# Splitting once and keeping the halves: latents and output weights of a two-layer attention encoder

## The chip, the cores and the metric

One core of a Trainium2 chip runs the whole program. The metric is device time in microseconds of one execution of the program. The median of three runs of the kernel before is 2840.68 us (2839.82 to 2844.84).

## The reference

Two layers run over 1024 prompt frames and 64 later frames with 256 frames of history, 1088 token rows in all, of width 1024. Everything is float32.

- Layer 0 projects the tokens once into a query latent (768 columns), a key-value latent (256), a rotary key (32) and band queries, keys and values. Both latents are RMS-normed. Eight heads attend over the latents (keys and values are projections of the key-value latent, with a chunk mask), eight heads attend over a band of nine chunks with a relative bias. The two outputs go through one output projection.
- Layer 1 is stick-breaking attention with 16 heads: each weight is a product of sigmoids over the later keys, with no softmax. Its output projection is w_out1.
- After each mixer: add and layer norm, a squared-ReLU feed-forward part of width 4096, add and layer norm.

```
h = x @ w_in
q_a = (rms_norm(h[:, :768], g_q) @ w_uq)       # query latent, then rotary on its last 32 per head
ckv = rms_norm(h[:, 768:1024], g_kv)           # key-value latent
k_a, v_a = ckv @ w_ukv                         # per head 64 key and 64 value columns
```

## The kernel before

**Products in three passes.** A float32 operand x is held as two tiles, H and L: H is x rounded to the matmul's format by a ScalarE copy, L is x minus H by VectorE (`split`, line 137). A product is H*H + H*L + L*H, three matmuls (`mm3`, line 141). Whatever enters a matmul has therefore been split once, by one instruction on each of ScalarE and VectorE. `weight` (line 163) loads one weight piece of up to 128 x 1024 into the single tile `wraw`, then splits it into one of two pairs, `wH0`/`wL0` and `wH1`/`wL1`, taken in turn. All transfers are issued by SyncE (SP), on one queue.

**Order of the work.** The program is written in order, and a planner with a model of the engines then places every engine's instructions; on the chip each engine runs its list strictly in that order. `paced` (line 528) adds ordering edges that the planner obeys but that are no semaphores on the chip.

**Stage 1, `latents` (line 294).** The nine token tiles (eight of 128 rows, one of 64), laid out with the features on the partitions, are loaded and split (`x_piece`); the weights of the key-value latent (`ck_piece`, four pieces) and of the query latent (`ql_piece`, eight) likewise. A first loop over the tiles projects the key-value latent, norms it, stores it as an output, turns it (three transposes), copies it out of PSUM into `stg` and stores it unsplit in the DRAM tensors `ck_d` and `krT_d`. A second loop does the same for the query latent in two halves of 384 columns, into `qn_d`. Then the constant rows of the rotary queries (`qconst`) are split and stored into `qr_d`, twelve transfers. The first band weight, w_bk of pair 0, is asked for inside the second loop.

**Stage 2, band attention.** For four pairs of heads, `heads64` (line 459) projects keys, queries and values of the next pair while `attend` works on the present one. During the last pair `load_latents` brings `qn_d` and `ck_d` back into SBUF, splits them, and splits the rotary key rows with their constants; the query projections (`rotate`, `nope`) fill TensorE's time beside the attention. `rotate` takes its cosine tile, and `parts` its split result, from the three buffers `raw`, which the loads of latents use too.

**Stage 3, latent attention.** `weight(io["w_mv"])` and the value projection come first; `proj_mla` (line 867) loads the key weights of one pair (128 x 256) and projects its keys, one pair ahead of the attention. During the last pair `out_early` (line 985) loads the eight blocks of w_out0, splits them and computes part of the output projection for some tiles.

**Stage 4** is the rest of layer 0 (output projection, feed-forward part). **Stage 5** is layer 1's attention: eight pairs by `heads64` and `row_stick` (line 590), whose chain goes from TensorE (scores) to ScalarE (two sigmoids), VectorE (a scan), GpSimd (a product), TensorE (a transpose), ScalarE and VectorE (split) and TensorE again. During the last pair, once x is released, `out_early` loads and splits w_out1. **Stage 6** is the rest of layer 1.

## Time and profile before

| | |
|---|---|
| median of three runs | 2840.68 us (2839.82 to 2844.84) |
| the profiled execution | 2842.44 us |
| its span, first to last instruction | 2840.6 us |
| TensorE busy | 2737.7 us, 96% |
| VectorE, ScalarE, GpSimd busy | 2160.4, 1512.2, 776.0 us |
| moved by DMA | 335.60 MB |

Stage 1 lasts until about 138 us, the band attention until about 430, layer 1's attention from about 1450 to 2050. PE is TensorE, PEld its weight loads, DVE VectorE, ACT ScalarE, POOL GpSimd, SP SyncE; SPq is SP's queue. L139 is line 139 of the kernel; that line is the subtract of `split`, so its tiles tell which split it is. In a row of groups stand the line, engine, operation and tiles (written<-read), shapes and count, then busy us and mean ns of one, then the engine's idle time before them with what ended it. A matmul's end is modelled, so the start-to-start distance is the better measure of its pace.

### The profile page before, as it was taken

Reading aid. Unit: us, or ns where it says so; the run is one execution under the profiler, and the core shown is the slowest. Engines: PE = TensorE matmul, PEld = TensorE weight load, DVE = VectorE, ACT = ScalarE, POOL = GpSimd, SP = SyncE. Lnnn points to the kernel's source line nnn. Section 1 sums busy time; section 2 is a strip of 40 time slices with the busy share of each in tenths; the row PEclk is TensorE's granted clock in tenths of the full one; section 3 lists DMA queues with packets and bytes.
Section 4 is the critical chain, followed back from the end, with each engine's and each line's share of the span. In section 5 each row is a group of like instructions: output and inputs, shape, how many; then the busy total and the mean of one; then the engine's idle time right before and its main releaser. Section 6 shows DMA issues by size and latency. Waiting matters only on the chain.

```text
span 2840.6 us, 46995 instructions
## 1 busy us (share of the span) xinstructions
PE 2737.7 (96%) x16907; PEld 2499.6 (88%) x16907; DVE 2160.4 (76%) x3837; ACT 1512.2 (53%) x3104; POOL 776.0 (27%) x890
## 2 busy tenths in 40 slices
PE   7999989999999999999999999998999999999998
PEld 7999978887899998878789999998879999977776
DVE  4266684885867777999978888888686777689998
ACT  4266664882555556333247777777445555543331
POOL 3123341652200002222533344344230000122235
PEclk9999999999999999999999999998999999999999
DMA  7122155334243447344231111113242444654442
GB/s 225 51 77 76 56 152 151 84 109 147 98 136 129 148 159 267 118 145 143 82 110 57 46 60 51 51 53 103 78 144 86 159 141 136 230 177 133 158 122 77
DMA packets 235752, 335.60 MB, mean 118 GB/s; under 512 B 45472, under 2 KB 168128, under 8 KB 235520
## 3 DMA queue, kind: packets, MB, share of 16 engines
q1 hardware_dynamic: 235520, 332.61, 37.2%
q8 instruction: 134, 2.20, 0.3%
q14 instruction: 98, 0.80, 0.1%
HBM read 217.83 MB, written 113.33 MB: 117 GB/s over the span
## 4 chain that ended last, share of the span: by engine, by line
PE 78%; DVE 9%; ACT 4%; DMA 4%; issue 3%; POOL 1%; SPq 0%; DVEq 0%; ACTq 0%; POOLq 0%
PE d L143 9%; PE d L144 9%; PE d L145 9%; PE s L143 5%; PE s L145 5%; PE s L144 5%; PE t L143 5%; PE t L144 5%; PE t L145 5%; PE t L161 4%; PE s L542 3%; PE pv L676 2%; PE pv L674 2%; PE pv L145 2%; PE pv L143 2%
## 5 line engine op out<-in xcount | busy, mean ns | idle before, releaser
L610 POOL TENSOR_TENSOR G<-G,S 128x384 f32<-128x384 f32 (+4 forms) x200 | 207.4, 1041 | 347.8 <-DVE S L607 128.4
L143 PE MATMUL d<-xH,wH 128*128 128x384 f32 (+1 forms) x792 | 266.4, 336 | 1.7 <-ACT kraw L509 1.6
L145 PE MATMUL d<-xH,wL 128*128 128x384 f32 (+1 forms) x792 | 264.0, 333 | 1.6 <-DVE wL L139 1.6
L144 PE MATMUL d<-xL,wH 128*128 128x384 f32 (+1 forms) x792 | 264.0, 333 | 0.0
L139 DVE TENSOR_TENSOR wtL<-t,wtH 128x512 fp32r<-128x512 f32 (+2 forms) x328 | 196.8, 618 | 54.3 <-ACT wtH L138 47.1
L138 ACT ACTIVATE wtH<-t 128x512 fp32r<-128x512 f32 (+2 forms) x328 | 170.6, 545 | 64.4 <-PE t L161 32.8
L549 POOL TENSOR_TENSOR R<-R,inv 128x640 f32<-128x640 f32 (+6 forms) x100 | 118.7, 1195 | 185.5 <-DVE inv L548 117.6
L674 PE MATMUL pv<-wtH,V 128*128 128x256 f32 (+1 forms) x624 | 159.3, 280 | 8.3 <-ACT o L634 4.0
L676 PE MATMUL pv<-wtL,V 128*128 128x256 f32 (+1 forms) x624 | 155.2, 289 | 7.0 <-DVE wtL L139 7.0
L143 PEld LDWEIGHTS d<-xH,wH 128*128 128x128 f32 x792 | 150.1, 190 | 5.4 <-ACT kraw L509 2.7
L607 DVE TENSOR_TENSOR_SCAN S<-S,own 128x513 f32<-128x513 f32 (+3 forms) x144 | 143.9, 1006 | 13.8 <-ACT S L600 12.2
L145 PEld LDWEIGHTS d<-xH,wL 128*128 128x128 f32 x792 | 149.9, 189 | 3.2 <-DVE wL L139 1.8
L144 PEld LDWEIGHTS d<-xL,wH 128*128 128x128 f32 x792 | 149.9, 189 | 1.0
L138 ACT ACTIVATE wo<-wo 128x1024 fp32r<-128x1024 f32 (+4 forms) x100 | 87.9, 883 | 113.9 <-DMA wo<-a_d 21.4
L674 PEld LDWEIGHTS pv<-wtH,V 128*128 128x128 f32 x624 | 120.1, 192 | 13.7 <-ACT o L634 6.3
L676 PEld LDWEIGHTS pv<-wtL,V 128*128 128x128 f32 x624 | 120.0, 192 | 10.8 <-DVE wtL L139 9.6
L161 PE MATMUL t<-ident,G 128*128 128x128 f32 x600 | 107.4, 282 | 12.6 <-POOL G L610 6.4
L542 PE MATMUL s<-kS,qH 128*128 128x384 f32 (+3 forms) x288 | 106.4, 372 | 4.9 <-ACT G L601 2.7
L600 ACT ACTIVATE S<-s 128x384 f32<-128x384 f32 (+4 forms) x200 | 99.1, 495 | 12.3 <-PE s L542 8.7
L601 ACT ACTIVATE G<-s 128x384 f32<-128x384 f32 (+4 forms) x200 | 100.1, 501 | 0.7 <-PE t L161 0.7
L139 DVE TENSOR_TENSOR wo<-wo,wo 128x1024 fp32r<-128x1024 f32 (+3 forms) x72 | 81.9, 1140 | 24.2 <-ACT wo L138 24.2
L542 PE MATMUL s<-kS,qL 128*128 128x384 f32 (+3 forms) x288 | 97.7, 341 | 0.0
(1724 smaller groups left out, 9836.0 us busy)
## 6 DMA issues: line engine op xcount, KB each, us to landing
wo<-a_d SPq DMA_DIRECT2D x53, 512.0 KB, 3.6
a_d<-wo SPq DMA_DIRECT2D x34, 544.0 KB, 4.2
sl<-a_d SPq DMA_DIRECT2D x29, 512.0 KB, 3.7
wo<-in_w_up SPq DMA_DIRECT2D x26, 512.0 KB, 4.1
wo<-in_w_dn SPq DMA_DIRECT2D x25, 512.0 KB, 5.4
sl<-in_w_dn SPq DMA_DIRECT2D x23, 512.0 KB, 6.3
xs<-a_d SPq DMA_DIRECT2D x19, 512.0 KB, 3.6
a_d<-sl SPq DMA_DIRECT2D x17, 544.0 KB, 5.0
```

Of the source, the lines that this page charges most:

```text
L138: self.nc.scalar.activation(H, src, AF.Copy)
L139: (engine or self.nc.vector).tensor_tensor(L, src, H.bitcast(F32), op=ALU.subtract)
L143: i = mm(out, aH, bH, start=first, stop=False)
L144: mm(out, aH, bL, start=False, stop=False)
L145: mm(out, aL, bH, start=False, stop=last)
L161: return self.nc.tensor.transpose(out, in_, self.ident[:n, :n])
L542: self.nc.tensor.matmul(ps[:, :n], q, k, start=i == 0, stop=i == len(passes) - 1)
L549: nc.gpsimd.tensor_tensor(R[:, :nk], R[:, :nk], inv.to_broadcast([P, nk]), op=ALU.mult)
L607: nc.vector.tensor_tensor_scan(s[r], s[r], own, carry, op0=ALU.mult, op1=ALU.max)
L610: nc.gpsimd.tensor_tensor(G[:, :n], G[:, :n], S[:, 1 : n + 1], op=ALU.mult)
L674: mm(out, v, wH[:, s : s + n], start=bi == 0 and s == 0, stop=False)
L676: mm(out, v, wL[:, s - n : s], start=False, stop=bi == len(banks) - 1 and j == bank[-1][0])
```

## The change

- **Latents split before they are stored.** In stage 1 the turned latents go from PSUM through `put_parts`: a ScalarE copy gives H, a VectorE subtract gives L, into the staging tiles `stgH` and `stgL` (two buffers each, where `stg` had three), and each half is stored. `qn_d` and `ck_d` become two tensors each, for H and L. `load_latents` then loads both halves straight into their tiles, with no split; only the cached latent is still split there. The rotary key keeps its own unsplit path, through a tile `krT`.
- **w_out1 split in stage 1.** For each of the first eight tiles of the second loop, `put_weights` loads 128 rows of w_out1, splits them by `weight`, and stores H and L in a new DRAM tensor `wo_d`. `out_early` of layer 1 loads the halves, two transfers of 512 KB a block, with no split and no raw slot. Layer 0 is as before.
- **Key weights of all pairs in one tile.** Four transfers fill one 128 x 1024 tile, one split serves the four pairs.
- **First transfers reordered.** x of tile 1 is loaded ahead of the loop and x of tile t+2 inside iteration t; w_ql pieces start one tile later. g_q, the w_out1 pieces, w_bk of pair 0, the qconst chunks and the other weights of pair 0 get an ordering edge (`after`) behind a chosen matmul of stage 1 (`marks`: the first matmul of the last k step of each full projection, eight for the key-value latents, then two per query tile). The edges are like those of `paced`: the planner's order, no semaphore.

```diff
+    def after(self, dma, mark):
+        if mark is not None:
+            self.tc.add_manual_dep(dma.ins, mark.ins.name, mybir.DependencyInfo(
+                mybir.DependencyClass.NoSync, mybir.DependencyReason.DATA), reason="pace")
...
+        def put_parts(dst, src, blocks, t0):
+            _, m, n = src.shape
+            parts = [self.tl(pa, [P, 3, P], f"stg{x}", 2, F32R)[:, :m, :n] for x in "HL"]
+            self.split(*parts, src)
+            for i in range(2):
+                nc.sync.dma_start(dst[i, :, blocks, t0 : t0 + n], parts[i].bitcast(F32))
+        def put_weights(k, mark):
+            src = io["w_out1"][k * P : (k + 1) * P, :].rearrange("p (a b) -> p a b", b=P)
+            parts = self.weight(src, [P, KD, P], mark)
+            for i in range(2):
+                nc.sync.dma_start(self.wo_d[k, i].rearrange("p (a b) -> p a b", b=P), parts[i].bitcast(F32))
...
         for k in (2, 4, 6):
             ck_piece(k)
+        x_piece(1)
...
-        gq = self.bcast(pa, io["g_q"], QL, "gq")
+        gq = None
         for t, (t0, n) in enumerate(TOK):
+            if t < 7:
+                x_piece(t + 2)
             if t:
-                x_piece(t)
-            if t < 8:
-                ql_piece(t)
+                ql_piece(t - 1)
...
-            stg = self.tl(pa, [P, 3, P], "stg", 3)
-            nc.scalar.activation(stg[:, :2, :n], tp[:, :2, :n], AF.Copy)
...
+            put_parts(self.ck_d, tp[:, :2, :n], slice(0, 2), t0)
...
+        gq = self.bcast(pa, io["g_q"], QL, "gq", marks[5])
         for t, (t0, n) in enumerate(TOK):
-            if t == 4:
-                first = self.weight(io["w_bk"][0], [P, KD, P])
+            if t < KD:
+                put_weights(t, marks[-1])
...
+                put_parts(self.qn_d, tp[:, :, :n], slice(3 * h, 3 * h + 3), t0)
+        first = self.weight(io["w_bk"][0], [P, KD, P], marks[-3])
         for c0, n in CHUNKS:
             qc = self.tl(pa, [ROPE, 384], "qc", 1)
-            nc.sync.dma_start(qc[:, :n], io["qconst"][:, c0 : c0 + n])
+            self.after(nc.sync.dma_start(qc[:, :n], io["qconst"][:, c0 : c0 + n]), marks[10])
...
-                    raw = qnL[s].bitcast(F32)
-                    nc.sync.dma_start(raw, self.qn_d[s])
-                    self.split(qnH[s], qnL[s], raw, nc.gpsimd if c0 >= 768 else None)
+                    for x, d in zip((qnH, qnL), (self.qn_d[0], self.qn_d[1])):
+                        nc.sync.dma_start(x[s].bitcast(F32), d[s])
...
+        mk = [x.rearrange("p (m a) b -> p m a b", m=4) for x in self.weight([io["w_mk"][m] for m in range(4)], [P, KD, P])]
...
-            w = self.weight(io["w_mk"][pair], [P, 2, P])
+            w = [x[:, pair] for x in mk]
...
-            raw = sl.take([D])
-            nc.sync.dma_start(raw, w[k * P : (k + 1) * P, :])
             ws[k] = [sl.take([D], F32R) for _ in "HL"]
-            self.split(*ws[k], raw)
-            sl.give(raw)
+            if layer:
+                for i in range(2):
+                    nc.sync.dma_start(ws[k][i].bitcast(F32), self.wo_d[k, i])
+            else:
+                raw = sl.take([D])
...
-        self.qn_d = tc.dram_tile([P, KQ, T], F32, name="qn_d")
-        self.ck_d = tc.dram_tile([P, 2, T], F32, name="ck_d")
+        self.qn_d = tc.dram_tile([2, P, KQ, T], F32, name="qn_d")
+        self.ck_d = tc.dram_tile([2, P, 2, T], F32, name="ck_d")
+        self.wo_d = tc.dram_tile([KD, 2, P, D], F32, name="wo_d")
```

More of the change, by code (lines that the diff above doesn't have):

```diff
@@ L457, in set64, with heads64 @@
         return qH, qL, qS, kS, V
[L459 removed]
+    def heads64(self, cp, bp, tiles, pair, w, cacheT, cache_v, outs, out0, cache_outs=(None, None), first=None, sooner=None):
         nc = self.nc
@@ L473, in step @@
             if kind not in ws:
-                ws[kind] = first if kind == "k" and first else self.weight(w[kind][pair], [P, KD, P])
+                ws[kind] = first if kind == "k" and first else self.weight(w[kind][pair], [P, KD, P], sooner)
                 if kind == "k":
```

57 lines of the change are left out of this document (30 added, 27 removed).

## The prediction

> **What bounds the kernel now.** The first part of the page and its chain of waits come first.
>
> ```profile
> span 2840.6 us, 46995 instructions
> ...
> PE 2737.7 (96%) x16907; PEld 2499.6 (88%) x16907; DVE 2160.4 (76%) x3837; ACT 1512.2 (53%) x3104; POOL 776.0 (27%) x890
> ...
> PE 78%; DVE 9%; ACT 4%; DMA 4%; issue 3%; POOL 1%; SPq 0%; DVEq 0%; ACTq 0%; POOLq 0%
> ```
>
> TensorE is busy for 96% of the span and makes 78% of the chain. The change removes no matmul, so it can win only where TensorE waits or where its clock is cut. The busy time by stretches shows these places; its columns are the stretch, its length, busy us (and instructions) of PE, PEld, DVE, ACT and POOL, then granted clock, DMA share, GB/s.
>
> ```profile
> 0.00:20.00 20.00, 9.54 (x43) 8.46 (x44) 8.03 (x9) 8.73 (x11) 0.76 (x8) 1.00 0.87 244
> 20.00:40.00 20.00, 16.82 (x128) 16.31 (x128) 12.10 (x20) 13.51 (x37) 14.29 (x38) 1.00 1.02 326
> 40.00:60.00 20.00, 15.74 (x105) 14.83 (x105) 9.49 (x16) 9.22 (x26) 5.41 (x24) 1.00 0.71 214
> 60.00:138.00 78.00, 78.00 (x470) 76.42 (x469) 14.66 (x39) 18.63 (x56) 9.74 (x18) 1.00 0.16 45
> ...
> 355.00:430.00 75.00, 61.88 (x379) 57.22 (x377) 59.13 (x149) 46.09 (x98) 31.96 (x27) 0.93 0.52 158
> 1971.00:2001.00 30.00, 20.10 (x84) 15.85 (x83) 28.50 (x31) 23.48 (x46) 13.68 (x21) 0.60 0.63 213
> 2001.00:2060.00 59.00, 59.00 (x326) 50.24 (x325) 36.42 (x52) 23.92 (x52) 15.19 (x26) 1.00 0.27 79
> ```
>
> Four readings. In the first 60 us TensorE is idle for 10.46 + 3.18 + 4.26 = 17.9 us while the DMA share is 0.87, 1.02 and 0.71: the transfers bound this stage. From 60 to 138 us (the query latents) TensorE is never idle and the DMA almost is: room for transfers. From 355 to 430 us 13.1 us are idle. From 1971 to 2001 us VectorE is full (28.50 of 30) and TensorE gets 20.10 busy us at a clock of 0.60, about 12.1 us of full-speed work: 18 us are lost. TensorE's waits in the first and the last of these stretches:
>
> ```profile
> PE d L143 <- ACT xH L138: 7.2, 1, 7.2
> PE s L143 <- ACT xH L138: 3.3, 2, 2.7
> PE s L143 <- ACT wqlH L138: 2.9, 1, 2.9
> ```
> ```profile
> PE pv L676 <- DVE wtL L139: 4.2, 2, 3.2
> PE t L161 <- POOL G L610: 3.8, 2, 2.4
> ```
>
> At the start it waits for operands just loaded and split, at 1971 us for VectorE's part of the attention.
>
> **Part 1, the first transfers.** What was moved in the first 60 us, and the rows of it that the change takes out or doubles (count, KB each, median us from issue to landing where there is one):
>
> ```profile
> DMA packets 17222, 15.68 MB, mean 261 GB/s; under 512 B 2048, under 2 KB 15168, under 8 KB 17216
> ...
> qr_d<-raw SPq DMA_DIRECT2D x8, 192.0 KB, 5.7
> ...
> ck_d<-stg SPq DMA_DIRECT2D x8, 128.0 KB, 3.7
> qr_d<-raw SPq DMA_DIRECT2D x4, 160.0 KB, 4.3
> wraw<-in_w_bk SPq DMA_DIRECT2D x1, 512.0 KB
> wraw<-in_w_bq SPq DMA_DIRECT2D x1, 512.0 KB
> wraw<-in_w_bv SPq DMA_DIRECT2D x1, 512.0 KB
> gq<-in_g_q SPq DMA_DIRECT2D x1, 384.0 KB
> ```
> ```profile
> 57.45 0.84 ACT L138 ACTIVATE wqlH<-praw 128x768 fp32r<-128x768 f32 x1 [0.49 <-DMA praw<-in_w_ql]
> ```
>
> Put behind marks, the three band weights (1.57 MB), the qr_d constants (2176 KB, 2.23 MB) and gq (0.39 MB) leave the stretch: 4.2 MB less. The second store of ck_d adds 1024 KB, 1.05 MB. So 12.5 MB stand where 15.7 stood, a ratio of 0.80. The last slice of w_ql starts its split at 57.45 us; scaled it would be 46, or 11.5 us sooner. From 40 us on the share is only 0.71, so not all of that is bytes: I take 9 us. Bounds: 0 (latency and two raw buffers set the pace, not bytes) and 13 of the 17.9 idle us. The copies from PSUM in put_parts become an ACT copy and a VectorE subtract; VectorE has 20 - 12.10 us free in its fullest stretch here and the nine new subtracts take about 0.4 us each (0.55 us for 384 columns, below): hidden.
>
> **Part 2, new work under the query projections.** One tile takes 94.87 - 85.89 = 8.98 us, read off the chain of waits; then the stores of the stretch 60 to 138 us, the price of a 512 KB split, and of a subtract from PSUM:
>
> ```profile
> 85.89 0.66 PE t L161 x6
> 94.87 0.66 PE t L161 x6
> ```
> ```profile
> qn_d<-stg SPq DMA_DIRECT2D x16, 192.0 KB, 2.1
> ```
> ```profile
> L139 DVE TENSOR_TENSOR wL<-wraw,wH 128x1024 fp32r<-128x1024 f32 x2 | 2.5, 1226 | 1.8 <-ACT wH L138 1.8
> L138 ACT ACTIVATE wH<-wraw 128x1024 fp32r<-128x1024 f32 x2 | 2.1, 1060 | 2.0 <-DMA wraw<-in_w_bq 1.5 <-DMA wraw<-in_w_bk 0.5
> ```
> ```profile
> 351.17 0.55 DVE L139 TENSOR_TENSOR V<-t,V 128x384 fp32r<-128x384 f32 x1
> ```
>
> put_weights adds per tile one load, 1.06 us ACT, 1.23 us VectorE and two stores; put_parts adds 2 x 0.55 us VectorE. Per tile that is 1.1 us more ACT and 2.3 us more VectorE, of 8.98; in 78 us VectorE was busy 14.66, so both are hidden. The traffic: eight times 1.57 MB, qn_d doubled to 6.9 MB, qr_d 2.2, band weights and gq 2.0: 23.7 MB in about 90 us, 263 GB/s, where 326 was moved from 20 to 40 us. It fits, at four fifths full. TensorE feels it only at the end: w_bk now loads behind marks[-3] (the end of tile 6), and through the single wraw behind the eighth put_weights. Two pieces, each about 5 us of landing (estimate, between 2.1 above and the 7.7 of a full burst below) plus 2.3 of split, are 14.6 us; tile 7 and the short tile 8 (32 of 48 passes) cover 8.98 + 6.0 = 15.0. At 7.7 us a landing it would be 20, a stall of 5. I take +2, bounds 0 and +8.
>
> **Part 3, loading the split latents.** VectorE's splits from 355 to 390 us, the loads of qn_d, and TensorE's largest waits from 350 to 430 us:
>
> ```profile
> L139 DVE TENSOR_TENSOR qnL<-qnL,qnH 128x1152 fp32r<-128x1152 f32 x4 | 6.3, 1570 | 0.3 <-ACT qnH L138 0.3
> ...
> L139 DVE TENSOR_TENSOR ckL<-raw,ckH 128x768 fp32r<-128x768 f32 (+2 forms) x5 | 3.6, 738 | 0.1
> ```
> ```profile
> qnL<-qn_d SPq DMA_DIRECT2D x4, 576.0 KB, 7.7
> ```
> ```profile
> PE d L143 <- ACT x L809: 3.4, 1, 3.4
> PE d L143 <- DVE raw L139: 2.0, 1, 2.0
> PE t L161 <- DVE wtL L139: 1.8, 1, 1.8
> ```
>
> VectorE sheds 6.3 us and four of the five ck splits (about 2.9), of 59.13 busy in 75; ACT sheds the matching copies. Against it stands twice the bytes (qn 6.7 MB instead of 3.3), and everything behind them on SP's queue (krT, kconst, ck_d, the next w_uq, the output stores) lands later; at the 380 GB/s that such a burst moves in the next part, 9 us later at most. The rotation's first operands need only the first four loads, which take as long as load and split did. The waits for x and raw (5.4 us) hang on the raw ring and the stores of qr_d, which stay. So of 13.1 idle us I take 4, bounds -10 and +3.
>
> **Part 4, w_out1 without its splits.** VectorE's groups from 1971 to 2001 us, then the rate (40 equal slices from 1965 to 2005 us) and landing of the loads:
>
> ```profile
> L139 DVE TENSOR_TENSOR wo<-wo,wo 128x1024 fp32r<-128x1024 f32 (+1 forms) x7 | 10.6, 1521 | 0.0
> ...
> L139 DVE TENSOR_TENSOR wo<-wH,wL 128x1024 fp32r<-128x1024 f32 x1 | 1.8, 1818 | 0.5 <-ACT wL L138 0.5
> ```
> ```profile
> GB/s 0 196 11 72 0 0 41 270 312 355 393 377 372 407 418 410 412 363 273 378 198 317 63 0 66 0 0 0 0 0 0 37 336 164 156 269 128 328 111 4
> ...
> wo<-in_w_out SPq DMA_DIRECT2D x6, 512.0 KB, 7.7
> ```
>
> Eight instructions, 12.4 us; one of them, 1.5 us by the mean, is the first token operand's and stays. So 11 us leave the engine that was the bound. The attention then has VectorE to itself. In their place come sixteen loads of 512 KB; three can start early in the five weight slots, thirteen (6.8 MB) when x is released near 1971 us. At about 390 GB/s they land 17 us later, near 1988, the token operand after them near 1993, against a first output matmul that comes at 2001 now. TensorE has no filling work until then. Of the 18 us lost I take 8; bounds 0 (output matmuls stand ahead of attention in TensorE's order and wait for the loads) and 16.
>
> The Trainium skill, "DMA: Bandwidth & Descriptors", section "Specifications", gives a core about 358 GB/s from HBM. The rows show 393 to 418 in single slices; by the page the thirteen loads take 19 us, and the sum would be 2 us worse.
>
> **Part 5, the key weights in one tile.** Four loads of 128 KB and four small splits become four loads and one split of 1.06 + 1.23 us, ahead of the first key projection. Two of the later ones leave the attention. I cost it at nothing; value matmuls cover the split, and uncovered it is 2.3 us.
>
> **The sum.** -9 + 2 - 4 - 8 = -19 us. The profiled execution took 2842.4 us, of which 2840.6 is the span; with the change 2823.4. The median shown, 2840.7, is 1.7 us below the profiled execution, so I forecast 2822 for the median.
>
> **Rivals.** (a) The attention at 1971 us is held by the loads: part 4 gives 0 and the time is 2830. For it: TensorE runs in written order, and 6.8 MB more come just there. Against: VectorE at 28.50 of 30. (b) The start is bound by latency, two raw buffers and splits, so part 1 gives 0: 2831. For it: the DMA share of 0.71 after 40 us; against: 1.02 before. (c) Slower: the staging ring of put_parts. Its two buffers, H and L, where stg had three, are each used again after two half tiles, 8.98 us. Copy and subtract take 1.1 us, so a store may take 7.9 us from readiness to landing; it took 2.1, but now stands on one queue behind 1.5 MB of put_weights per tile. Above 7.9 us every half tile stalls for half the excess, through the transposes' banks. At 11.5 us that is 1.8 us for each of 17 half tiles, 31 us: sum +12, 2853. It outweighs the rest from 10.1 us on. Against it: the four-fifths load. (d) The change doesn't do what it says: the marks order only the planner's list and are no semaphores, so transfers can go out at other moments than meant, and the plan shifts elsewhere: 2841.
>
> **How the numbers follow.** Forecast 0.55, (a) 0.15, (b) 0.15, (c) 0.09, (d) 0.06. The range goes from 2806 (bounds -13, 0, -9, -12) to 2838, which leaves out (c), most of (d) and little below. What this kernel's runs can tell from no change is 0.2%, 5.7 us. Faster: 0.55 + 0.13 + 0.12 = 0.80. Same: 0.02 of (a), 0.03 of (b), 0.04 of (d) = 0.09. Slower: 0.09 + 0.02 = 0.11.
>
> **What would show it.** Part 1: the last split of w_ql starts near 48 us and TensorE's idle time before 60 us falls to about 9. Part 2: tiles still 9 us apart, and a wait for wH of at most 5 us where the key projection starts. Part 3: no splits of qn, and less idle between 370 and 390 us of before. Part 4: no 1024-column splits at the end of layer 1's attention, the first output matmul some 5 us sooner, and a clock above 0.60 there. I am wrong if tiles are over 10 us apart, if TensorE waits for a load in layer 1's last pair, or if idle time merely moves to the next stage.

## The result, and the profile after

| | before | after |
|---|---|---|
| median, five runs each on one chip | 2842.00 us (2839.82 to 2848.15) | 2860.39 us (2857.02 to 2863.94) |
| profiled execution, its span | 2842.44, 2840.6 us | 2857.02, 2855.2 us |
| moved by DMA | 335.60 MB | 361.31 MB |

The ratio is 1.0059, with a 95% interval from 1.0046 to 1.0072: the changed kernel is 0.6% slower, about 17 us, where 19 us less were forecast. The first part of its page and its chain of waits:

```profile
span 2855.2 us, 47131 instructions
...
PE 2744.0 (96%) x16907; PEld 2504.9 (88%) x16907; DVE 2165.2 (76%) x3853; ACT 1504.4 (53%) x3091; POOL 771.3 (27%) x888
...
PE 73%; DVE 11%; ACT 5%; DMA 4%; issue 4%; POOL 1%; SPq 1%; DVEq 0%; ACTq 0%; POOLq 0%
```

The same matmuls, 6 us more of busy time for them, and a chain in which TensorE's share fell from 78% to 73%. The stretches that the prediction read (layer 1's end shifted by the 20 us that everything there is late):

```profile
0.00:20.00 20.00, 11.95 (x76) 11.38 (x76) 8.53 (x9) 9.35 (x11) 0.77 (x8) 1.00 0.80 245
20.00:40.00 20.00, 17.63 (x131) 16.45 (x130) 14.42 (x27) 13.64 (x38) 17.14 (x42) 1.00 0.90 269
40.00:60.00 20.00, 18.94 (x116) 17.82 (x116) 8.86 (x20) 7.65 (x27) 5.91 (x22) 1.00 0.83 248
60.00:138.00 78.00, 69.17 (x405) 66.97 (x404) 30.61 (x59) 26.17 (x62) 3.85 (x7) 0.98 0.83 251
355.00:430.00 75.00, 61.50 (x354) 57.21 (x353) 48.86 (x145) 38.38 (x90) 23.75 (x25) 0.84 0.63 194
1991.00:2022.00 31.00, 21.95 (x127) 18.03 (x125) 29.00 (x36) 22.84 (x53) 17.61 (x33) 0.88 0.77 278
2022.00:2080.00 58.00, 57.90 (x279) 48.50 (x280) 30.30 (x41) 17.83 (x35) 11.21 (x12) 0.94 0.35 104
```

TensorE's idle time before 60 us fell from 17.9 to 11.5 us, but 8.8 us of idle time are new between 60 and 138 us, where there was none. From 355 to 430 us the idle time hardly moved (13.1 to 13.5 us) while the granted clock fell from 0.93 to 0.84.

**Where the time went.** The table below is worked out from the traces. For a moment of the before profile, take the time at which the other kernel's TensorE has begun the same share of its matmul columns (20 added for each matmul), and subtract. Each column is what that difference gained over a stretch of the before profile (-340 is the stretch from 150 to 340 us); minus is time won, and the last column is the whole. Each row is one profiled execution.

| kernel | 0-65 | -150 | -340 | -455 | -485 | -690 | -1375 | -1485 | -1945 | -2060 | -end | sum |
|---|---|---|---|---|---|---|---|---|---|---|---|---|
| after | -7.9 | +11.1 | 0.0 | +9.7 | -4.2 | +1.2 | +1.0 | +9.5 | +0.9 | -5.3 | -1.5 | +14.6 |
| e1, the same lists again | -8.8 | +11.6 | 0.0 | +8.5 | -4.2 | +1.6 | +0.4 | +7.8 | +1.2 | -5.6 | +0.7 | +13.3 |
| e2, slot order back | -8.2 | +12.1 | 0.0 | +8.8 | +4.6 | +3.3 | -0.2 | +5.0 | 0.0 | -5.7 | +1.8 | +21.5 |
| e3, unsplit latents | -9.1 | +5.8 | +1.6 | +10.3 | -4.2 | +0.6 | +0.5 | +8.5 | +2.3 | -6.5 | +2.7 | +12.5 |
| e4, first transfers only | -6.4 | 0.0 | 0.0 | +6.5 | +1.4 | +2.1 | +1.2 | -0.2 | +1.0 | +0.4 | +0.7 | +6.5 |
| e5, splits pinned | -7.5 | +16.0 | +1.6 | +8.3 | -4.2 | +1.7 | -0.4 | +9.2 | -0.1 | -8.2 | +2.1 | +18.5 |
| e6, no stored weights | -6.2 | +0.5 | 0.0 | +8.9 | -4.1 | -0.2 | +1.3 | +7.0 | +1.5 | +5.2 | +1.9 | +15.9 |
| e7, keys only | +2.4 | 0.0 | 0.0 | +0.8 | +1.7 | +3.0 | +2.6 | +3.7 | +1.4 | +4.9 | -3.5 | +16.9 |
| e8, slots only | +2.7 | 0.0 | 0.0 | +0.5 | -0.1 | +7.8 | -0.2 | +5.9 | +0.8 | -3.9 | +2.4 | +16.0 |
| e9, marks only | -8.7 | 0.0 | 0.0 | +10.4 | +0.8 | +0.6 | +0.5 | 0.0 | +0.6 | -0.4 | +0.6 | +4.4 |
| e10, order only | -1.1 | 0.0 | 0.0 | +7.3 | -0.3 | 0.0 | +1.1 | -0.2 | +1.8 | -2.9 | -2.8 | +2.9 |
| e11, stored in a flat stage | +2.6 | 0.0 | 0.0 | +2.2 | -0.8 | +0.4 | +0.9 | +0.1 | +40.6 | -5.8 | -3.7 | +36.4 |
| e12, slices ahead only | +1.1 | 0.0 | +2.2 | +4.0 | +0.8 | +0.3 | +0.5 | -0.2 | +0.4 | -2.4 | -2.8 | +4.0 |
| e13, two marks | -5.4 | 0.0 | +1.4 | +2.8 | -0.8 | +0.1 | +0.9 | -0.2 | +0.2 | -2.9 | 0.0 | -3.8 |
| e14, factors' mark | -5.0 | 0.0 | 0.0 | +0.8 | -0.3 | -0.8 | +0.5 | 0.0 | +0.3 | -3.0 | +0.1 | -7.3 |

Read the first row as the result: three gains (the start, the keys near 480 us, layer 1's last pair) and three losses of 9.5 to 11.1 us each. e1 has the same lists as the changed kernel: its row differs from the first by 2.2 us at most, and a column is good to about that; between 340 and 455 us two executions of the same lists (e4 and e9) differ by 3.9. The rows e7, e8 and e11 leave the first stage as before and are 2.4 to 2.7 us late at 65 us. The before profile was a lucky one: 2842.44 us, where the medians of its kernel below are 1.5 to 3.7 us longer.

### The profile page after: what moved, and what is told of

Its sections match the earlier page's. It is cut to its first block, busy times and chain, and to the rows that moved or that the text cites. A ratio compares the mean times of both kernels' runs of the same rounds, so it can differ in the third digit from the quotient of the medians.

```text
span 2855.2 us, 47131 instructions
## 1 busy us (share of the span) xinstructions
PE 2744.0 (96%) x16907; PEld 2504.9 (88%) x16907; DVE 2165.2 (76%) x3853; ACT 1504.4 (53%) x3091; POOL 771.3 (27%) x888
## 2 busy tenths in 40 slices
DMA packets 253498, 361.31 MB, mean 127 GB/s; under 512 B 47856, under 2 KB 181776, under 8 KB 253264
## 4 chain that ended last, share of the span: by engine, by line
PE 73%; DVE 11%; ACT 5%; DMA 4%; issue 4%; POOL 1%; SPq 1%; DVEq 0%; ACTq 0%; POOLq 0%
PE d L143 9%; PE d L144 9%; PE d L145 8%; PE t L144 5%; PE t L143 5%; PE t L145 5%; PE s L145 5%; PE s L143 5%; PE s L144 5%; PE t L161 4%; PE s L569 3%; PE pv L703 2%; PE pv L701 2%; PE pv L145 2%; PE pv L143 2%
## 5 line engine op out<-in xcount | busy, mean ns | idle before, releaser
L138 ACT ACTIVATE wo<-wo 128x1024 fp32r<-128x1024 f32 (+4 forms) x91 | 80.1, 883 | 110.4 <-DMA wo<-a_d 17.2
L139 DVE TENSOR_TENSOR wL<-wraw,wH 128x1024 fp32r<-128x1024 f32 (+1 forms) x52 | 65.0, 1251 | 74.9 <-ACT wH L138 73.2
L189 POOL TENSOR_TENSOR rr<-rv,mhalf 128x1 f32<-128x1 f32 (+1 forms) x54 | 34.4, 640 | 242.5 <-DVE rv L187 138.3
```

Source lines behind the costliest of these rows:

```text
L138: self.nc.scalar.activation(H, src, AF.Copy)
L139: (engine or self.nc.vector).tensor_tensor(L, src, H.bitcast(F32), op=ALU.subtract)
```

## The experiments

Times are medians; the before kernel ran beside each group (2843.98, 2846.14, 2844.09 and 2844.57 us).

### What stalls the query latents: e1, e3, e5, e6

In the changed kernel TensorE waits 8.8 us between 60 and 134 us, each time for a normed latent, and ScalarE 36.9 us for the blocks of w_out1 (views of waits, of TensorE and of ScalarE; total, times, longest):

```profile
PE t L161 <- DVE qn L426: 8.8, 3, 5.5
```
```profile
ACT wH L138 <- DMA wraw<-in_w_out: 36.9, 6, 9.5
```

The token tiles drift apart, 8.98, 9.98, 11.88 and 16.55 us from one to the next (timeline of TensorE), and ScalarE stands still ahead of the copies of the blocks (its timeline; in brackets the idle time before the instruction and what ended it):

```profile
59.89 0.82 PE L161 MATMUL t<-ident,qn 128*128 128x128 f32 x6
68.87 0.82 PE L161 MATMUL t<-ident,qn 128*128 128x128 f32 x6
78.85 1.04 PE L161 MATMUL t<-ident,qn 128*128 128x128 f32 x6 [0.84 <-DVE qn L426]
90.73 1.04 PE L161 MATMUL t<-ident,qn 128*128 128x128 f32 x6 [2.52 <-DVE qn L426]
107.28 1.51 PE L161 MATMUL t<-ident,qn 128*128 128x128 f32 x6 [5.46 <-DVE qn L426]
```
```profile
60.12 1.06 ACT L138 ACTIVATE wH<-wraw 128x1024 fp32r<-128x1024 f32 x1 [5.04 <-DMA wraw<-in_w_out]
73.45 1.06 ACT L138 ACTIVATE wH<-wraw 128x1024 fp32r<-128x1024 f32 x1 [9.47 <-DMA wraw<-in_w_out]
...
95.95 1.06 ACT L138 ACTIVATE wH<-wraw 128x1024 fp32r<-128x1024 f32 x1 [7.56 <-DMA wraw<-in_w_out]
```

ScalarE takes its list in order. The squares of the tile, without which no latent is normed, stand behind a copy whose block has not landed. The blocks are late because of what stands between them on SP's queue. The subtract of the block copied at 60.12 us frees `wraw` at 62.45 us, but the next load goes out at 66.81 us, behind the two stores of halves and four of the qr_d stores that Part 1 moved into this stage; when those are through, the load goes out 0.4 us after the subtract (98.28 and 98.69 us). So Parts 1 and 2 met on one queue. e6 below shows that the qr_d stores alone do no harm there; no run has the blocks without them.

**e1** moves the split behind the tile in the source.

```diff
-            if t < KD:
-                put_weights(t, marks[-1])
+            rest = put_weights(t, marks[-1]) if t < KD else None     # only the load
...
                 put_parts(self.qn_d, tp[:, :, :n], slice(3 * h, 3 * h + 3), t0)
+            if rest is not None:
+                rest()                                               # split and stores
```

> The changed kernel with one thing moved: of each output weight block of layer 1 the transfer in is still issued ahead of its token tile, but its two split instructions and the two stores come after that tile's latents are stored, not ahead of its projection. The bytes, the queue and the number of instructions are the same. Theory (ScalarE takes its list in order, and the copy of a block that has not landed stands at the head of it, so the squares and the staging copies behind it are late and TensorE waits for the normed latents): the progress of TensorE at the end of the query-latent stage, which fell from 8 us ahead of the kernel before to 3 us behind it, stays ahead by 5 to 8 us, the gaps on the transposes of the normed latents (2.5 us near 91 us and 5.5 us near 107 us) go, and the time is 9 to 11 us under the changed kernel's 2860, about 2850. Rival (the transfers themselves: the eight blocks in and sixteen halves out crowd the queue that also stores the split latents): the gaps stay, and the time is within 3 us of 2860. Rival (c) of the prediction (the two-deep staging ring of the split halves): gaps stay too, and stand at the staging copies behind their stores.

2859.83 us, ratio 1.0053 (1.0038 to 1.0068): no change, where about 2850 was expected, and for a reason that no theory had. The build wrote the same list for every engine, row for row, as for the changed kernel. Where a line stands in the source didn't decide where it runs. The run is so a second measurement of the changed kernel, 0.6 us from the first.

**e5** holds the two instructions back by ordering edges as well.

```diff
+            def rest(done):                       # done: the tile's last copy and subtraction
+                for i, j in zip(self.split(*parts, raw), done):
+                    self.after(i, j)
```

> The changed kernel with the two split instructions of each stored block of layer 1's output weights held, in the lists that the build writes, behind the second staging copy and subtraction of the same token tile (moving them in the source alone left every engine's list as it was, row for row). Bytes, queue and instruction counts are the same. Theory (ScalarE's list: the copy of a block that has not landed stands ahead of the squares and staging copies of the tile): ScalarE's idle stretches of 5 to 9 us in front of those copies go, the 11 us that TensorE loses between 60 and 110 us shrink to 3 or less, its progress at 340 us is 5 to 8 us ahead of the kernel before (3 behind in the changed kernel), and the time is 2850 to 2856, since the crowded stage at 345 to 430 us gave back 6 us of such a lead before. Rival (the queue: eight blocks in, sixteen halves out and the doubled latent stores are simply more than it moves in that time): the loss of 11 us stays, and the progress at 340 us is within 2 us of the changed kernel's.

2860.92 us, ratio 1.0050 (1.0035 to 1.0065), where 2850 to 2856 was expected. ScalarE's idle time ahead of the copies shrinks and then ends, and at 107 us TensorE is 3.2 us ahead of before where the changed kernel is 3.2 behind: of the 11.1 us, 4.3 are still lost by then. But by 150 us e5 is 8.5 us behind. The copies come once a tile now, 9 us apart, and the first band key weight stands ninth in that row:

```profile
87.17 1.06 ACT L138 ACTIVATE wH<-wraw 128x1024 fp32r<-128x1024 f32 x1 [3.40 <-DMA wraw<-in_w_out]
...
110.72 1.06 ACT L138 ACTIVATE wH<-wraw 128x1024 fp32r<-128x1024 f32 x1
...
128.87 1.06 ACT L138 ACTIVATE wH<-wraw 128x1024 fp32r<-128x1024 f32 x1
137.91 1.06 ACT L138 ACTIVATE wH<-wraw 128x1024 fp32r<-128x1024 f32 x1 [3.56 <-DMA wraw<-in_w_bk]
```
```profile
PE t L161 <- DVE qn L434: 8.2, 3, 4.7
PE s L143 <- ACT wH L138: 5.0, 1, 5.0
```

With no band weight TensorE has nothing to fill the gaps with. It waits 4.7 us for the last tile's latents, at 132.90 us, and 5.0 us for the weight, at 139.02.

So both theories hold a part. The copy at the head of ScalarE's list made most of the stall between 70 and 110 us; with that reduced, the single tile `wraw` makes one at 128 to 139 us, since eight blocks at one a tile fill the stage and the band weight has to wait for its turn.

**e6** leaves out the stored halves, and **e3** the split latents (and splits them in `load_latents` as before):

```diff
-            if t < KD:                                                                       # e6; out_early of
-                put_weights(t, marks[-1])                                                    # layer 1 as before
-            parts = [self.tl(pa, [P, 3, P], f"stg{x}", 2, F32R)[:, :m, :n] for x in "HL"]    # e3
-            self.split(*parts, src)
-            for i in range(2):
-                nc.sync.dma_start(dst[i, :, blocks, t0 : t0 + n], parts[i].bitcast(F32))
+            stg = self.tl(pa, [P, 3, P], "stg", 3)[:, :m, :n]
+            nc.scalar.activation(stg, src, AF.Copy)
+            nc.sync.dma_start(dst[0, :, blocks, t0 : t0 + n], stg)
```

> The changed kernel without the stored halves of layer 1's output weights: nothing of them is loaded, split or stored under the query latents, and layer 1's early output projection loads and splits the blocks as the kernel before does. The split latents, the key weights in one tile and the first transfers stay as changed. Theory: TensorE loses nothing between 60 and 110 us (progress at 340 us 7 to 8 us ahead of the kernel before, as in the first-transfers-only run), the stage at 345 to 455 us still loses some 10 us, the 5 us won in layer 1's last pair are gone, and the time is 2852 to 2858. Rival (the split latents' doubled stores hold that stage by themselves): 3 us or more of the 11 stay.

> The changed kernel, but the latents are stored unsplit (one transfer a half tile) and split when they are loaded, as in the kernel before; all else as changed. Theory (twelve loads of query latents where six stood put everything behind them on the queue some 10 us later: the rotation's factors, the position keys, the cached latents; ScalarE and VectorE then run the rotations later and TensorE waits): the 11 us lost between 340 and 455 us go, and the time is 9 to 12 us under 2860, about 2850. Rival (the loss there comes from something else, as the rotation waiting for the copies of the query factors made in the first stage): it stays, and the time is within 3 us of 2860. If in addition the query-latent stage gets faster, the doubled stores of the halves had a part in the stall there.

e6: 2857.74 us, 1.0037 (1.0024 to 1.0051), as expected. The 11.1 us lost between 65 and 150 us become 0.5, and layer 1's last pair is 10.5 us worse than in the changed kernel (+5.2 against -5.3): against e6 the stored halves win there about what they cost here. e3: 2854.19 us, 1.0034 (1.0019 to 1.0048), where about 2850 was expected. In the query latents it loses 5.8 us instead of 11.1. With half of the latents' stores gone the blocks come faster: from copy to copy 11.3, 11.1 and 8.9 us pass where the changed kernel has 13.3, 11.9 and 10.6, and ScalarE waits 5.6 us for blocks instead of 36.9. The doubled stores alone (e6) cost 0.5 us, so the two parts together cost more than the sum of either. But between 340 and 455 us e3 loses 10.3 us with unsplit latents, as much as with split ones. My theory of that stage, that twelve loads instead of six make everything behind them late, falls.

### What is lost between 340 and 455 us: e4, e9, e10, e12, e13, e14

**e4** is the kernel before with only the reordered first transfers, the diff of `x_piece`, `ql_piece` and every `after`, as shown with the change (it also has the tile `krT` and, like the changed kernel, one tile for the squares where before has two).

> The kernel before with only the first transfers reordered and paced (token slices two tiles ahead, query weights a tile later, the later weights and factors marked to follow named matmuls), and with the staging and square tiles as that needs; no split latents in memory, no stored halves of layer 1's weights, key weights pair by pair, slot order of before. Theory: the 8 us that TensorE is ahead at 52 us in the changed kernel are kept to the end, 2842 less 8 to 9, about 2833.5. Rival (an early gain is given back at a later transfer, as most of that in layer 1's last pair was): within 3 us of 2842.

2849.15 us, 1.0021 (1.0012 to 1.0031): slower, by its ratio, where about 2833.5 was expected. The lead of 6.4 us at 65 us is kept to 340 us, and 6.5 us are lost by 455 us. Two explanations were left: the lead runs into work that ends at a fixed time, or the stage is a different one. Comparing the order of the engines' instructions spoke for the second. A planner places the instructions by its own model of the whole program, and the edit in the first stage had changed TensorE's list where nothing was edited. The table counts the places in TensorE's order (16,907 matmuls in all) at which the traces have another matmul than before's, by its tiles and shape; the columns go by before's time:

```
kernel                     to 155 us   155-420 us   420-1950 us   from 1950 us
e4  first transfers only      141         1185            6           271
e9  marks only                143         1185            6           271
e10 order only                140         1193           27           199
e12 slices ahead only         103         1031           55           199
e13 two marks                 119           27            0            95
e14 factors' mark             114           27            0            95
e7  keys only                   0            0          865           369
e8  slots only                  0            0         2783            92
```

From 155 us on e4 and e9 have the same order on TensorE, VectorE, ScalarE and GpSimd, and so have e13 and e14; e10 parts from e4 only at 387 us. Before, e7, e8 and e11 have the same order up to 455 us.

**e9** has only the marks of `after`, **e10** only the new order, **e12** only the slices of x two tiles ahead.

```diff
+            if t < 7:                                                               # e10, e12; x of tile 1
+                x_piece(t + 2)                                                      # ahead of the loop
             if t:
-                x_piece(t)
-            if t < 8:
-                ql_piece(t)
+                ql_piece(t - 1)                                                     # e10; e12 keeps t
...
-        gq = self.bcast(pa, io["g_q"], QL, "gq")                                # e9: marks, old order
+        gq = self.bcast(pa, io["g_q"], QL, "gq", marks[5])                      # ahead of the second loop
-                first = self.weight(io["w_bk"][0], [P, KD, P])
+                first = self.weight(io["w_bk"][0], [P, KD, P], marks[-1])
-            nc.sync.dma_start(qc[:, :n], io["qconst"][:, c0 : c0 + n])
+            self.after(nc.sync.dma_start(qc[:, :n], io["qconst"][:, c0 : c0 + n]), marks[10])
```

> The kernel before with only the later weights and factors marked to follow named matmuls (gain row, first band key and query weights, query factors); the token slices and query weight pieces are issued in the order of before. From about 140 us on the build gives every engine the same list as in the first-transfers-only run, which differs from the list before between 290 and 430 us. Theory (the lists): TensorE's progress at 340 us is within 3 us of the kernel before, since nothing is won at the start, and yet the stage from 340 to 455 us loses 5 to 7 us, so about 2850. Rival (the 6 us lost there in the first-transfers-only run were the lead itself, met by work that ends at a fixed time whatever TensorE does): nothing is lost there, since there is no lead, and the time is within 3 us of the kernel before.

> The kernel before with only the order of the first transfers changed (token slices two tiles ahead, query weight pieces one tile later), no marks. Its lists between 140 and 350 us are those of the first-transfers-only run. Theory: TensorE is 5 to 9 us ahead at 52 us and keeps it up to 340 us (or somewhat less, since the factors and gain rows still go in early), then loses 5 to 7 us by 455 us; about 2842 to 2848. Rival (the marks, not the order, brought the early gain): no lead at 52 us.

> The kernel before with only the token slices issued two tiles ahead, the query weight pieces and all else as before. The build then writes yet another list for 200 to 430 us. Theory (a list is a draw, and that of before is a good one): a lead of some us at 52 us, and a change between 340 and 455 us that differs from the 6 us of the first-transfers-only run; within 6 us of 2844 in all. Rival (a lead at the start is always lost in that stage): the lead at 340 us and the loss by 455 us are equal within 2 us.

e9: 2844.69 us, 1.0003 (0.9994 to 1.0012). e10: 2846.47 us, 1.0016 (1.0007 to 1.0026). e12: 2850.35 us, 1.0023 (1.0014 to 1.0033). Three of my expectations were misses: e9 has a lead of 8.7 us at 340 us, e10 one of 1.1, and e12 none (3.4 us late), so the marks clear the queue for the first stage, not the order of the slices. But e4, e9 and e10, with leads of 6.4, 8.7 and 1.1 us and practically one list, lose 6.5, 10.4 and 7.3 us: the loss doesn't go with the lead. What it consists of is in the stage's own rows, before (340 to 455 us), e9 and the changed kernel (the same work, 331.3 to 456.8 and 343.3 to 468.1 us):

```profile
340.00:455.00 115.00, 101.88 (x634) 96.44 (x633) 73.55 (x179) 59.41 (x126) 35.52 (x32) 0.96 0.51 151
```
```profile
331.30:456.80 125.50, 110.91 (x636) 106.21 (x636) 73.47 (x179) 59.52 (x127) 36.97 (x33) 0.88 0.48 139
```
```profile
343.30:468.10 124.80, 108.18 (x636) 102.66 (x636) 62.28 (x171) 51.45 (x117) 28.76 (x31) 0.89 0.59 179
```

TensorE is idle for 13.1 us before and 14.6 in e9. Of 10.5 us more, 1.5 are idle time and 9.0 are the same matmuls at a lower clock, 0.88 instead of 0.96. In the changed kernel it is 3.5 us idle and 6.3 at a clock of 0.89, and in e4, which has e9's lists, 2.9 idle and 3.7 at 0.93: how the loss divides varies from one execution to the next. In e9's middle the clock is at half for 10 us and more:

```profile
380.00:385.00 5.00, 3.25 (x19) 2.88 (x19) 5.00 (x14) 2.75 (x6) 1.29 (x2) 0.84 0.01 3
385.00:390.00 5.00, 4.03 (x20) 3.84 (x19) 4.81 (x19) 4.39 (x13) 4.37 (x5) 0.50 0.44 106
390.00:395.00 5.00, 5.00 (x21) 5.00 (x22) 4.71 (x11) 1.62 (x5) 2.67 (x3) 0.50 0.39 87
```

A copy stands at the head of ScalarE's list here again, this time of the next piece of w_uq, whose load stands on SP's queue behind four stores of the rotation. In e9 (e4 has the same row with 6.33 us) and, the copy that takes its place, in before:

```profile
412.12 0.84 ACT L138 ACTIVATE wH<-wraw 128x768 fp32r<-128x768 f32 x1 [6.45 <-DMA wraw<-in_w_uq]
```
```profile
410.52 0.86 ACT L138 ACTIVATE wH<-wraw 128x768 fp32r<-128x768 f32 x1
```

e10 waits 1.0 us there and loses 7.3 us all the same, so this row isn't the whole cause, and what in the list costs the time stays open.

**e13 and e14** then needed a variant with a lead and before's own list. Two smaller sets of the marks have it, but for a few matmuls (the table of lists): the mark on the query factors alone (e14), and with it that on the second and third band weights (e13).

```diff
-            nc.sync.dma_start(qc[:, :n], io["qconst"][:, c0 : c0 + n])                       # e13, e14
+            self.after(nc.sync.dma_start(qc[:, :n], io["qconst"][:, c0 : c0 + n]), marks[10])
...
-                ws[kind] = first if kind == "k" and first else self.weight(w[kind][pair], [P, KD, P])   # e13
+                ws[kind] = first if kind == "k" and first else self.weight(w[kind][pair], [P, KD, P], sooner)
```

> The kernel before with two marks of the change alone: the query factors (and so their twelve broadcast stores) follow a named matmul of the query-latent stage, and the second and third weights of the first band pair follow the last of them that latents() marks. The token slices, the query weight pieces, the gain row and the first band key weight go as before. Unlike the three first-transfer runs, the build then leaves TensorE's list as before's from 145 us to 1980 us. Theory (the lists, not the lead, decide what the stage from 340 to 455 us costs): a lead of 3 to 9 us at 107 us against the runs that have the list of before in the first stage, kept within 2 us through 455 us and to the end; 2844 less 3 to 9, about 2838, faster than both kernels. Rival (the lead is lost in that stage because work there ends at a fixed time): the lead is gone by 455 us and the time is within 2 us of the kernel before.

> The kernel before with one mark of the change alone, that of the query factors; the band weights are loaded as early as before. TensorE's list is before's from 145 us to 1980 us here too. Theory: a part of the lead (2 to 6 us at 107 us), kept through 455 us and to the end; 2838 to 2842. Rival (fixed time): gone by 455 us, within 2 us of the kernel before.

e13: 2837.45 us, 0.9977 (0.9966 to 0.9989). e14: 2839.17 us, 0.9976 (0.9967 to 0.9985). Both are faster than both kernels. With before's list the stage costs e14 0.8 us and e13 2.8 us; e7, e8 and e11, which have that list and no lead, 0.8, 0.5 and 2.2. With the other lists it costs 4.0 to 10.4. So it is the list. A part of the lead may be lost besides: e13 also gave up 1.4 us between 150 and 340 us, so its lead was not kept within the 2 us expected. And not all of the time won is the lead: 3.0 of e14's 7.3 us come from layer 1's last pair, where 95 matmuls stand in other places. The first rows of e14's page:

```profile
span 2833.3 us, 46995 instructions
...
PE 2737.4 (97%) x16907; PEld 2499.1 (88%) x16907; DVE 2155.7 (76%) x3837; ACT 1511.2 (53%) x3104; POOL 784.2 (28%) x890
```

### The layers' boundary and the keys: e2, e7, e8

The first weight of layer 1, w_ck, is issued into `wraw` at 1420.52 us before; after, only when that slot's last tile is stored (timelines of SP, before and after, and the changed kernel's wait):

```profile
1420.52 0.33 SPq L169 DMA_DIRECT2D wraw<-in_w_ck  x1
```
```profile
1462.07 0.32 SPq L282 DMA_DIRECT2D x_d<-wraw  x1
1466.31 0.33 SPq L179 DMA_DIRECT2D wraw<-in_w_ck  x1
```
```profile
PE d L143 <- ACT wH L138: 4.9, 1, 4.9
```

The edit of `out_early` takes the halves' slots before the raw one in layer 0 too, and the free slots include the five weight tiles. **e8** makes that edit alone in the kernel before, **e2** takes it back in the changed kernel, **e7** has only the key weights in one tile (the diff shown with the change).

```diff
-            raw = sl.take([D])                                    # e8
-            nc.sync.dma_start(raw, w[k * P : (k + 1) * P, :])
             ws[k] = [sl.take([D], F32R) for _ in "HL"]
+            raw = sl.take([D])
+            nc.sync.dma_start(raw, w[k * P : (k + 1) * P, :])
```

> The kernel before with only the order of slots changed in layer 0's early output projection (the two halves' slots taken ahead of the raw block's), which moves no work. Theory (slots): the first weight of layer 1 is issued near 1460 us where it was 1420 us, TensorE waits some 5 us for it, and the time is 6 to 10 us over 2844, about 2852. Rival (the loss at the layers' boundary came from the later start of everything, not from the slots): within 3 us of 2844, that weight still issued near 1420 us.

> The changed kernel, but layer 0's early output projection takes the slot of the raw weight block ahead of the two slots of its halves again, as the kernel before does; nothing else. Theory (the changed order shifts every later choice of a slot up to the end of layer 0, so that the slot which layer 1's first weight needs is held by a late tile and its transfer is issued 46 us later than before): the first weight of layer 1 is issued again near 1420 us plus the shift of the stages ahead of it, the loss of about 7 us at the start of layer 1 goes and some of the 3 us in the feed-forward ahead of it, and the time is 7 to 10 us under 2860, about 2851. Rival (layer 1's weight is late because the whole of layer 0's end is later or slower at a lower clock): no change, within 3 us of 2860.

> The kernel before with only the key weights of the four latent pairs in one tile. Theory: the wait of 4 us ahead of the keys near 480 us goes as in the changed kernel (5.6 us won between 455 and 485 us) and is kept: 2844 less 4 to 6, about 2839. Rival (the build sorts every engine's list anew for any edit, and what a stage wins or loses by that is as large as the edit's own effect): the time lands anywhere within 6 us of 2844, and TensorE's progress changes by several us in stages that the edit does not touch.

e8: 2859.88 us, 1.0046 (1.0029 to 1.0062). It moves no work and costs 14 us, where 6 to 10 were expected. 5.9 of the 14 us are the boundary, by the mechanism expected:

```profile
1458.62 0.32 SPq L272 DMA_DIRECT2D x_d<-wraw  x1
1462.87 0.33 SPq L169 DMA_DIRECT2D wraw<-in_w_ck  x1
```
```profile
PE d L143 <- ACT wH L138: 4.8, 1, 4.8
```

Another 7.8 us went between 485 and 690 us, and 5.0 of them in one wait (below). e2: 2864.38 us, 1.0071 (1.0056 to 1.0086), slower than the changed kernel, where 2851 was expected, although w_ck goes out at 1440.97 us again, as expected, and the boundary costs 5.0 us instead of 9.5. e7: 2860.37 us, 1.0052 (1.0037 to 1.0067), 14 us over its before kernel, where 4 to 6 under it were expected. Near 480 us, where the changed kernel won 4.2 us, e7 lost 1.7 and e2 4.6. The wait that the edit was to remove, in before, and what TensorE waits for in its place in e7 and e2:

```profile
PE d L542 <- DVE mx L582: 3.9, 1, 3.9
```
```profile
PE d L545 <- DVE k1L L139: 4.6, 1, 4.6
```
```profile
PE d L569 <- DVE k1L L139: 7.6, 1, 7.6
```

VectorE's half of the keys waits for ScalarE's, and ScalarE for a load (timelines of ScalarE, e7, e2 and e8):

```profile
484.14 1.06 ACT L138 ACTIVATE wL<-wH 128x1024 fp32r<-128x1024 f32 x1 [6.53 <-DMA wH<-in_w_out]
485.23 0.59 ACT L138 ACTIVATE k1H<-d 64x512 fp32r<-64x512 f32 x1
```
```profile
496.63 1.06 ACT L138 ACTIVATE wL<-wH 128x1024 fp32r<-128x1024 f32 x1 [9.49 <-DMA wH<-in_w_out]
497.71 0.59 ACT L138 ACTIVATE k1H<-d 64x512 fp32r<-64x512 f32 x1
```
```profile
558.27 1.06 ACT L138 ACTIVATE wraw<-wL 128x1024 fp32r<-128x1024 f32 x1 [5.27 <-DMA wL<-in_w_out]
```

It is the first block of w_out0 for the early projection of layer 0. With the keys' weights taken in one piece, a weight tile falls free early, the block's load goes out at 477.18 us in e7 and at 489.55 in e2 (511.87 us before), and its copy is put ahead of the keys'. The changed kernel differs from e2 only in the order of slots, which gives that block another place; its first load of w_out0 goes out at 591.76 us. In e8 the same copy stands ahead of an output that TensorE needs, at 560 us:

```profile
PE pv L674 <- ACT o L634: 5.0, 1, 5.0
```

So the two edits help each other near 480 us and each costs some 14 us alone: parts of a change don't add up here. Near the boundary e7 loses 3.7 us; one call of `weight` for four turns the pair that w_ck falls on, which may be why, but no run tells.

### Storing the halves elsewhere: e11

```diff
             self.paced(steps, marks, 2 if pair < 7 else -3)
+            for i in range(2 if 0 < pair < 5 else 0):            # layer 1, pairs 1 to 4
+                k = 2 * pair - 2 + i
+                src = self.io["w_out1"][k * P : (k + 1) * P, :].rearrange("p (a b) -> p a b", b=P)
+                parts = self.weight(src, [P, KD, P], marks[3 + 3 * i])
+                for j in range(2):
+                    nc.sync.dma_start(self.wo_d[k, j].rearrange("p (a b) -> p a b", b=P), parts[j].bitcast(F32))
```

> The kernel before with only the stored halves of layer 1's output weights, made not under the query latents but under layer 1's pairs 1 to 4 (two blocks a pair, from about 1560 to 1800 us), where TensorE has no wait; the early projection loads the halves as in the changed kernel. Theory (the stall was made by where the blocks were put, not by the work): nothing is lost between 1560 and 1900 us, layer 1's last pair is 4 to 6 us shorter between 1945 and 2017 us as in the changed kernel, and the time is 2 to 6 us under the kernel before if the new lists cost nothing elsewhere. Rival (sixteen halves stored and loaded back cost more than the splits they save): slower in those two stretches together.

2878.96 us, 1.0123 (1.0107 to 1.0138). The last pair is 5.8 us shorter, as expected, and 40.6 us are lost between 1485 and 1945 us, where the theory had none. TensorE from 1560 to 1945 us of before, and over the same work in e11:

```profile
1560.00:1945.00 385.00, 373.59 (x2510) 359.86 (x2509) 322.09 (x467) 283.71 (x679) 155.99 (x291) 1.00 0.17 53
```
```profile
1565.40:1991.00 425.60, 393.11 (x2511) 371.57 (x2510) 341.07 (x477) 293.21 (x691) 163.79 (x290) 0.94 0.24 77
```

21 us more idle, 20 us more busy at a clock of 0.94. The loss comes in four steps of some 9 to 13 us, one in each of the four pairs that take blocks, and in each the clock is at half for 6.8 to 13.7 us. VectorE was busy for 322 of 385 us there, which I had not counted. Whether eight splits on a nearly full VectorE or the new list (1912 places of TensorE's order differ between 420 and 1950 us) did it, no run tells.

## Why the prediction was wrong

The forecast of 2822 us lies 38 us under the median, outside the range. By its own steps:

- **Part 1 (-9): right.** The last split of w_ql starts at 44.99 us ("near 48", the row is below), TensorE's idle time before 60 us is 11.5 us ("about 9"), and the lead at 65 us is 7.9 us against the before profile and 10 to 11 against e7, e8 and e11, which have its first stage. The bytes set the pace: e9, which only moves transfers out of the stage, has the gain, and e10, which only changes the order, has not. Rival (b) falls.
- **Part 2 (+2, at most +8): mis-sized, and the step that failed is "in 78 us VectorE was busy 14.66, so both are hidden".** Busy sums say how much room an engine has, not whether its list can reach it. It cost 11.1 us, mostly through a copy that waits for its block at the head of ScalarE's list. "Tiles are over 10 us apart" was the sign I had named; they are up to 16.6. The other limit, the turn of `wraw`, was in the working, at the right place and up to 5 us, and showed when the first was reduced (5.0 us in e5).
- **Part 3 (-4): wrong.** VectorE shed 11.3 us of busy time between 340 and 455 us (73.55 to 62.28), more than forecast, and TensorE's idle time there rose from 13.1 to 16.6 us: it did not hang on those splits. The loads neither won nor lost (9.7 us against 10.3 with unsplit latents). The doubled stores cost some 5 us in stage 1, beside the blocks; "It fits, at four fifths full" held for bytes and not for the moment at which a block lands.
- **Part 4 (-8): 5.3 against before.** The splits are gone and the clock rose from 0.60 to 0.88, as the mechanism has it. How much of the gain is theirs stays open: e6, without the halves, is 10.5 us worse, but e8, e10, e12, e13 and e14, which store no halves either, win 2.4 to 3.9 us there by their other lists. The loads landed in 10.0 us instead of 7.7. TensorE waits for no load in that pair, and its longest wait from 1991 us on, 3.2 us, is for GpSimd, so rival (a) falls. The first output matmul came at 2025.72 us, which is 2.9 us later than before once the 21.4 us at 1945 us are taken off, not 5 sooner; of 7.3 us won by 1985 us, 2.0 were given back by 2060.
- **Part 5 (0):** -4.2 us in the changed kernel, where the wait of 3.9 us went, and +1.7 alone. That tiles fall free earlier was not asked.
- **Not in the sum: the slots of layer 0.** The diff takes them in another order, and the text ahead of the prediction says that layer 0 is as before. The boundary cost 9.5 us, of which e8 gives 5.9 to the slots alone; e7, the key weights alone, loses 3.7 there.
- **Rival (d) was the one that decided, and was priced at nothing.** "The plan shifts elsewhere: 2841" had a chance of 0.06. A shifted plan cost 4 to 10 us between 340 and 455 us, 7.8 us in e8, 9 us between two kernels near 480 us. Rival (c), the nearest in time, fell: ScalarE waits for weight blocks, and no wait of it from 60 to 134 us is for a store of the staging buffers; a latent's store took 2.5 us from issue to landing.
- **The range** was narrower than the working. Its lower end takes -9 and -12 where Parts 3 and 4 state -10 and -16, and its upper end leaves out the +8 of Part 2 and the +3 of Part 3. With the stated bounds it would run from 2802 to 2852, and the result would still lie outside. (The doubled qn_d is 6.7 MB, as Part 3 has it, not 6.9; nothing hangs on that.)

So of the 34 us between the forecast for the profiled execution and its time, 9 are Part 2, 14 the stage at 340 to 455 us (where -4 stood), 9.5 the boundary, 3 Part 4 and 1 the start; Part 5 gave 4 back, and the small columns are the rest.

Rows of the changed kernel for this list: the last split of w_ql, the first output matmul of layer 1, the latents' stores (count, KB each, median us to landing), and, for layer 1's end, the rate in 40 slices of 1 us from 1985 us on and the landing of the halves:

```profile
44.99 0.84 ACT L138 ACTIVATE wqlH<-praw 128x768 fp32r<-128x768 f32 x1 [2.33 <-DMA praw<-in_w_ql]
```
```profile
2025.72 0.78 PE L143 MATMUL d<-wraw,wo 128*128 128x512 f32 x1
```
```profile
qn_d<-stgH SPq DMA_DIRECT2D x14, 192.0 KB, 2.5
```
```profile
GB/s 6 66 0 37 266 307 348 328 327 397 400 435 406 418 422 406 414 414 418 393 414 411 341 329 378 331 322 371 78 60 5 0 66 0 0 0 0 66 0 0
...
wo<-wo_d SPq DMA_DIRECT2D x11, 512.0 KB, 10.0
```

Thirteen slices are at 393 to 435 GB/s. The Trainium skill, "HBM Reference", section "Specifications (TRN2)", gives about 425 GB/s for a core that streams alone. This program runs on one core, and the rows lie near that figure, not at the 358 GB/s that I drew on, which that section gives as the share when both cores of a pair stream.

## What to carry to other kernels

Room on an engine is not cover: of each instruction that is added or freed to go earlier, ask what it waits for and what stands behind it in its engine's list; a copy whose load hadn't landed, at the head of ScalarE's list, cost TensorE 8.8 us in the query latents, 4.6 and 7.6 near 480 us (e7 and e2) and 5.0 near 560 us (e8). Where a planner orders the lists, an edit changes tight stages that it doesn't touch, so compare the lists ahead of the run and look for the form of the edit that leaves them as they were (e14 against e4: one mark instead of the set, 7 us faster than before instead of 6 slower, by the ratios). And where buffers are handed on, ask who gets the slot next.

## What the runs showed of the hardware

- **A microsecond of idle can cost several.** In e9, between 340 and 455 us of before, 1.5 us more idle time came with 9.0 us more of busy time (in e4, with the same lists, 2.9 with 3.7). The clock was 0.50 from 385 to 395 us, although no gap of TensorE between 360 and 400 us was over 1.4 us. The Trainium skill, "TensorE: Matmul & The Clock Gate", section "HAM oscillation — how this bites in real kernels", has as its rule no idle gaps over about 3.4 us; here many short ones were enough, as its section "A second HAM failure mode: psum-queue depth-cycling" describes for another kernel.
- **The start of one and the same list varies by up to 2.7 us.** e7, e8 and e11 are 2.4 to 2.7 us late at 65 us against before, whose lists they have there. In all three the clock is at half for 3.4 us from about 54 us on, and in before it is not; by my estimate that alone is 1.7 us, half of 3.4. So a term of 2 us, as I had summed one, can't be read from one profile of a start.
